# Scaling the S5 products of the output projection inside PSUM, and listing both attention outputs ahead of the recursion's second half

## The chip, the cores and the metric

The kernel runs on one core of a Trainium2 chip. The metric is the device time of one execution in microseconds (us); smaller is better. Each time below is of this one core.

## The reference, cut to what matters

A two-layer decoder trunk: 272 tokens (16 meta tokens and 256 inputs) of width 1024, float32. Each layer adds to the residual h half a SwiGLU, then a mixer, then half a SwiGLU again. The mixer projects the normalised h with `w_in`, and three groups of heads work on the columns:

- attention (256 columns): stick-breaking weights, then `o_sb = rmsnorm(weights @ v)` per head of 64;
- gated DeltaNet (256 columns): a chunked recursion over chunks of tokens, normalised per head and gated;
- S5 (512 columns): a diagonal state space model, a gate (GLU), and one rmsnorm over its 512 columns.

The three are concatenated and multiplied with `w_out` (1024 x 1024), and the product is added to h. Rows 0 to 255 of `w_out` thus belong to attention, 256 to 511 to DeltaNet and 512 to 1023 to S5. A row's rmsnorm is one factor for each token, so S5's may be applied after the product with `w_out` as well as before it.

## The kernel before, in words

Everything lies transposed: features on the 128 partitions, tokens along the free dimension. The residual is `xT` (8 blocks of 128 features by 272 tokens); the operand of each projection is held as a high and a low part, `xh` and `xl`, and the weights as `wh` and `wl`, and each product is three matmuls (`mm3`, L134 to L138): high by high (L136), low by high (L137), high by low (L138). A weight block of 512 KB is loaded by SP (L128), ScalarE makes `wh` (L130) and VectorE `wl` (L131); there are 3 buffers for the raw block, 3 for `wh` and 2 for `wl` (`NBUF`, L44).

The mixer (L1340) is a list of steps, `MIX` (L42 and L43), that the loop at L1429 walks through. It traces the instructions in this order. The framework's planner then puts them into the engines' queues by when it expects them to be ready, the earlier listed first among those that are, so a matmul listed later can stand ahead of one listed earlier that is not ready. Each queue runs in order. Buffers have tags: PSUM has four (`a` to `d`) of 2 banks each, and `cv` is an SBUF tag of 3 buffers (L857).

The letters of the list that matter here:

- `r`: one stage of the DeltaNet recursion (`dn_rest`, L1079). Stages 1 to 3 make its operands. Stages 4 and 5 are the first chunk: `pvn` (L1148), its copy (L1150), `pS` (L1154 and L1156). Stage 6 is `pk` of the second chunk (L1138 and L1139), which VectorE reads (L1142 to L1144). Stage 7 is the second chunk's `pvn` and copy, stage 8 its `pS` and the update on VectorE (L1163 to L1165), stages 9 to 11 the last 16 tokens (`pkt` L1171, `pvt` L1179 and L1183). From stage 4 on all of them use PSUM tag `d`.
- `a`: one stage of attention (`sb`, L1220). The last two are `outputs(0)` and `outputs(1)` (L1266 to L1282): six matmuls into a `d` bank (`pob`), their squares `sbr` on ScalarE (L1274), two matmuls that sum them (`pnb`, tag `c`, L1276), a root (ScalarE L101 twice, then three VectorE instructions in `newton`, L115 to L117), the scaled result `sby` (L1279) and its parts in `xh` and `xl` (L1281 and L1282). `sbr` and `sby` are `cv` buffers; the `d` bank is held until L1279 has read it.
- `x`: one half of S5's gate (`glu`, L1290). `m`: S5's factor `R5`, from a matmul of its sum of squares (`pms`, L380, tag `b`) and a root.
- `n`: ScalarE's table for Exp and Ln is loaded.
- `S4`, `S6`, `S0`, `S2`: S5's 512 rows of `w_out` for a pair of feature blocks each (`w_out_part("S", ...)`, L1402): 24 matmuls into two banks (tag `a` for S4 and S0, `b` for S6 and S2); then for each bank `sy` = product times `R5` (L1418) and its addition to `xT` (L1420).
- `o`: DeltaNet's norm and output: squares (L1191), their sum (L1193), a root, the scaled `o` (L1198), transposes `po` (L1210), `dy` (L1213 and L1215), `xh` (L1216) and `xl` (L1217) of two blocks.

After the list the four parts `Y4`, `Y6`, `Y0`, `Y2` follow (the same function with "Y"): each first the rows of attention for both banks (12 matmuls), then the rows of DeltaNet (12 more), then the addition to `xT`, from which the next SwiGLU's operand is split at once (L357).

Of the kernel before, what the change touches and what calls it, by code (L numbers as in the profile page):

```python
# [14 lines left out]
ALU = mybir.AluOpType  # L15
# [6 lines left out]
T = NMETA + SEQ  # L22
# [17 lines left out]


MIX = "C2 C3 U0 g U1 g g U2 g g g U3 g Q0 p0 p1 Q1 t0 p2 p3 K0 i t1 K1 a a t2 C0 a a i C1 i t3 a a i C4 i a a i C5 l i " \  # L42
      "y0 V0 i y1 V1 i y2 Z0 y3 Z1 v r r r r x r r x r n a r r r r a m S4 S6 o S0 S2"  # L43
NBUF = (3, 2, 3)  # L44
LO_POOL = 5

# [13 lines left out]
class Trunk:  # L60
# [1279 lines left out]
    def mixer(self, l, nxt):  # L1340
        nc, a = self.nc, self.a
        V, G, A, PE = nc.vector, nc.gpsimd, nc.scalar, nc.tensor
        w_in, w_out = a["w_in"][l], a["w_out"][l]
        t0 = NMETA if l == DEPTH - 1 else 0
        self.norm_end()
        R = self.R
        with ExitStack() as es:
            self.tmp = tmp = es.enter_context(self.tc.tile_pool(name="mix", bufs=1, reuse_waits="tile"))
            qkv = tmp.tile([P, 6, TP], F32, name="qkv")
            G.memset(qkv[:, :, T:], 0.0)  # L1350
            ba = tmp.tile([8, TP], F32, name="ba")
            G.memset(ba[:, T:], 0.0)

            def conv(b):
                src = w_in[:, 768 + b * P:768 + b * P + P]
                if b == 2:
                    p, pb = self.unit([(src, 0, P), (w_in[:, 1792:1800], P, P + 8)], P + 8, "ab")
                    V.tensor_tensor(ba[:, :T], pb[:8, :T], R[:8], op=ALU.mult)
                else:
                    p, = self.unit(src, P)  # L1360
                pad, y = self.cv("pad"), qkv[:, b, :T]
                G.memset(pad[:, 0:3], 0.0)
                V.tensor_tensor(pad[:, 3:3 + T], p[:, :T], R, op=ALU.mult)
                A.activation(y, pad[:, 0:T], AF.Copy, scale=self.cw[:, l, 0, b:b + 1])
                for k in range(1, 4):
                    V.scalar_tensor_tensor(y, pad[:, k:k + T], self.cw[:, l, k, b:b + 1], y, op0=ALU.mult, op1=ALU.add)
                if b in (2, 3):
                    self.act(y, y, AF.Silu)

            u = tmp.tile([P, 4, T], F32, name="s5u")  # L1370
            zr = tmp.tile([P, 2, T], F32, name="pz")
            q, k, v = (tmp.tile([P, 2, T], F32, name=f"p{n}") for n in "qkv")

            def s5_in(b):
                p, = self.unit(w_in[:, 1800 + b * P:1800 + b * P + P], P, "ba"[b % 2])
                i = lambda t: t.rearrange("p (c j) -> p c j", j=4)
                V.tensor_tensor(u[:, b, :].rearrange("p (j c) -> p c j", j=4), i(p[:, :T]), i(R), op=ALU.mult)

            def proj(c0, dst, b):
                p, = self.unit(w_in[:, c0 + b * P:c0 + b * P + P], P)  # L1380
                V.scalar_tensor_tensor(dst[:, b, :], p[:, :T], 0.125 if c0 == 0 else 1.0, R, op0=ALU.mult, op1=ALU.mult)

            def do_z(b):

                proj(1536, zr, b)
                t = self.cv("zt")[:, :T]
                self.act(t, zr[:, b, :], AF.Tanh, scale=0.5)
                V.scalar_tensor_tensor(zr[:, b, :], t, 1.0, zr[:, b, :], op0=ALU.add, op1=ALU.mult)

            def silu():  # L1390
                self.phase(SET_SILU)
                for b in (0, 4):
                    self.act(qkv[:, b:b + 2, :T], qkv[:, b:b + 2, :T], AF.Silu)
                self.phase(SET_GELU)

            def norms():
                self.phase(SET_LNEXP)


            rows = dict(S=((4, 5, 6, 7),), Y=((0, 1), (2, 3)))  # L1400

            def w_out_part(x, d0, tag):  # L1402
                ks = rows[x]
                lo = min(k for g in ks for k in g)
                n = sum(len(g) for g in ks)
                ps = [self.psum(tag[i % len(tag)], "proj") for i in range(2)]
                h, w = self.weights(w_out[lo * P:(lo + n) * P, d0 * P:d0 * P + 256], n, 256)
                for g in ks:
                    for j in range(2):
                        js = slice(j * P, j * P + P)  # L1410
                        for k in g:
                            self.mm3(ps[j][:, :T - t0], h[:, k - lo, js], w[:, k - lo, js],
                                     self.xh[:, k, t0:], self.xl[:, k, t0:], k == ks[0][0], k == ks[-1][-1])
                for j in range(2):
                    x_, p = self.xT[:, d0 + j, t0:], ps[j][:, :T - t0]
                    if x == "S":
                        y = self.cv("sy")[:, :T - t0]
                        V.tensor_tensor(y, p, self.R5[:, t0:], op=ALU.mult)  # L1418
                        p = y
                    V.tensor_tensor(x_, p, x_, op=ALU.add)  # L1420

            chains = dict(g=self.dn_gates(l, qkv, ba), i=self.dn_inverse(), r=self.dn_rest(qkv),
                          a=self.sb(l, q, k, v, 0), x=self.glu(l, u))
            steps = dict(C=conv, U=s5_in, Q=lambda b: proj(0, q, b), K=lambda b: proj(256, k, b), V=lambda b: proj(512, v, b),
                         Z=do_z, p=lambda r: self.s5_inputs(u, r), t=self.s5_states, y=lambda r: self.s5_outputs(u, r),
                         l=silu, v=lambda: self.sb_values(), n=norms, S=lambda d0: w_out_part("S", d0, "ab"[d0 // 2 % 2]),
                         o=lambda: (self.dn_norm(), self.dn_out(zr, self.dng[:, l], 2)),
                         m=lambda: self.rms(self.acc, 4 * 512, 0, self.R5, "b"))
            for x in MIX.split():  # L1429
                if x in chains:  # L1430
                    next(chains[x], None)
                else:
                    steps[x[0]](*(int(n) for n in x[1:]))
            assert all(next(c, 0) == 0 for c in chains.values())
            self.norm_begin(*nxt)
            for d0 in (4, 6, 0, 2):
                w_out_part("Y", d0, "ab"[d0 // 2 % 2])
                for d in {4: (4, 5), 6: (6, 7), 0: (), 2: (0, 1, 2, 3)}[d0]:
                    self.norm_block(d, d0 == 2, t0)
            self.blocks = (4, 0)  # L1440
# [42 lines left out]
```

## Time and profile before

| | before |
|---|---|
| median of 3 runs | 1169.95 us (1167.01 to 1170.87) |
| the profiled execution | 1172.42 us |
| its span in the trace | 1170.6 us |
| TensorE busy (PE) | 98% of the span |
| VectorE busy (DVE) | 73% |
| ScalarE busy (ACT) | 53% |
| mean granted TensorE clock | 0.98 of 2.4 GHz |

The profile shows one execution. PE is TensorE's matmuls, PEld its weight loads, DVE is VectorE, ACT is ScalarE, SP issues the loads from memory. A row of a timeline gives the start, the duration, engine, line, operation, what it writes and reads, the shape, how many instructions are merged in it, and in brackets how long the engine stood idle before it and what ended that. In a table of windows each engine has its busy time and its count of instructions. PEclk is the clock that TensorE was granted, as a share of 2.4 GHz: its two levels are 1.2 and 2.4 GHz, and a value between them is a mean over a stretch. The span between the trace's ends is 1.8 us shorter than the execution's own time.

### The profile page before, as it was taken

The numbers are of one execution on the slowest core, as the hardware profiler recorded it, in microseconds if no ns is written. First come the engines' busy times: TensorE is split into PE (matmuls) and PEld (weight loads), VectorE is DVE, ScalarE is ACT, GpSimd is POOL, SyncE is SP. The second block draws the span as 40 slices with busy tenths as digits, with TensorE's granted clock in tenths as the row PEclk, the third lists the DMA queues.
The fourth block names the chain that finished last, engine by engine and source line by source line (L and its number), as shares of the span: only waits on it lengthen the run. The fifth ranks groups of instructions, "written<-read, shape, count | busy, mean of one in ns | idle before, by whom it ended". The sixth has DMA issues, their size and how long they took to land.

```text
span 1170.6 us, 23740 instructions
## 1 busy us (share of the span) xinstructions
PE 1141.7 (98%) x9544; PEld 1094.8 (94%) x9544; DVE 849.4 (73%) x1621; ACT 621.7 (53%) x993; POOL 164.0 (14%) x230
## 2 busy tenths in 40 slices
PE   7999999999998999999999999999999989999997
PEld 7999999998996999999999999999989969999985
DVE  6999987589646965555569998756995578666544
ACT  6455466474653654444445555654655637555533
POOL 6411111102200011110201111011031001111100
PEclk9999999999988999999999999999999879999999
DMA  6656654642311556665566566456432216666663
GB/s 185 172 165 183 171 157 138 180 127 72 92 55 55 145 170 174 179 180 163 185 173 176 164 182 177 136 167 167 109 91 74 79 41 198 187 183 183 196 194 111
DMA packets 196859, 173.75 MB, mean 148 GB/s; under 512 B 21300, under 2 KB 193004, under 8 KB 196748
## 3 DMA queue, kind: packets, MB, share of 16 engines
q1 hardware_dynamic: 196732, 172.22, 50.4%
q8 instruction: 75, 1.23, 0.4%
q14 instruction: 36, 0.29, 0.1%
q10 hardware_dynamic: 16, 0.00, 0.0%
HBM read 171.15 MB, written 1.05 MB: 147 GB/s over the span
## 4 chain that ended last, share of the span: by engine, by line
PE 87%; DVE 6%; ACT 2%; POOL 2%; DMA 1%; issue 1%; SPq 0%; ACTq 0%; DVEq 0%; POOLq 0%
PE proj L138 18%; PE proj L136 18%; PE proj L137 18%; PE pd L138 5%; PE pd L137 5%; PE pd L136 5%; PE pd L485 5%; DVE wl L131 1%; PE pY L842 1%; POOL t L1004 1%; PE pm L775 1%; PE pinc L808 1%; PE pob L1270 1%; POOL TT L1005 1%; PE pY L840 1%
## 5 line engine op out<-in xcount | busy, mean ns | idle before, releaser
L136 PE MATMUL proj<-xh,wh 128*128 128x272 f32 (+1 forms) x1840 | 525.2, 291 | 0.8 <-DVE sy L1418 0.8
L137 PE MATMUL proj<-xl,wh 128*128 128x272 f32 (+1 forms) x1840 | 521.1, 289 | 0.0
L131 DVE TENSOR_TENSOR wl<-raw,wh 128x1024 fp32r<-128x1024 f32 (+1 forms) x324 | 392.7, 1212 | 147.2 <-PE pd L138 58.6
L138 PE MATMUL proj<-xh,wl 128*128 128x272 f32 (+1 forms) x1840 | 493.9, 291 | 2.5 <-DVE wl L131 2.3
L130 ACT ACTIVATE wh<-raw 128x1024 fp32r<-128x1024 f32 (+1 forms) x324 | 338.3, 1044 | 290.2 <-PE proj L137 86.0
L136 PEld LDWEIGHTS proj<-xh,wh 128*128 128x128 f32 x1840 | 348.8, 190 | 3.5 <-DVE sy L1418 1.6
L137 PEld LDWEIGHTS proj<-xl,wh 128*128 128x128 f32 x1840 | 348.6, 190 | 1.7
L138 PEld LDWEIGHTS proj<-xh,wl 128*128 128x128 f32 x1840 | 331.7, 189 | 5.2 <-DVE wl L131 4.0
L136 PE MATMUL pd<-hh,wh 128*128 128x272 f32 x528 | 149.6, 288 | 0.0
L137 PE MATMUL pd<-hl,wh 128*128 128x272 f32 x528 | 149.3, 288 | 0.0
L427 POOL TENSOR_TENSOR hl<-h,hh 128x272 fp32r<-128x272 f32 (+1 forms) x88 | 80.0, 911 | 455.4 <-ACT hh L426 455.3
L138 PE MATMUL pd<-hh,wl 128*128 128x272 f32 x528 | 140.7, 288 | 0.2
L136 PEld LDWEIGHTS pd<-hh,wh 128*128 128x128 f32 x528 | 99.2, 188 | 0.2
L137 PEld LDWEIGHTS pd<-hl,wh 128*128 128x128 f32 x528 | 99.2, 188 | 0.1
L138 PEld LDWEIGHTS pd<-hh,wl 128*128 128x128 f32 x528 | 95.1, 188 | 0.9 <-DVE wl L131 0.8
L101 ACT ACTIVATE g<-g 128x272 f32<-128x272 f32 (+2 forms) x92 | 37.7, 414 | 66.0 <-DVE g L421 65.7
L426 ACT ACTIVATE hh<-h 128x272 fp32r<-128x272 f32 (+1 forms) x88 | 36.4, 419 | 48.0 <-DVE h L425 48.0
L425 DVE TENSOR_TENSOR h<-proj,g 128x272 f32<-128x272 f32 (+1 forms) x88 | 37.8, 433 | 32.3 <-PE proj L138 20.8
L421 DVE TENSOR_TENSOR g<-proj,R 128x272 f32<-128x272 f32 (+1 forms) x88 | 37.5, 430 | 17.6 <-PE proj L138 17.5
L423 DVE TENSOR_TENSOR g<-g,R 128x272 f32<-128x272 f32 (+1 forms) x88 | 38.1, 436 | 13.0 <-ACT g L101 12.6
L368 POOL TENSOR_TENSOR acc<-acc,sq 128x272 f32<-128x272 f32 (+1 forms) x20 | 22.5, 1123 | 93.1 <-ACT sq L362 92.4
L485 PE MATMUL pd<-wh,hl 128*128 128x512 f32 x80 | 31.7, 396 | 0.0
(489 smaller groups left out, 1242.0 us busy)
## 6 DMA issues: line engine op xcount, KB each, us to landing
raw<-in_ffn_w_gate_dram SPq DMA_DIRECT2D x88, 512.0 KB, 3.9
raw<-in_ffn_w_up_dram SPq DMA_DIRECT2D x88, 512.0 KB, 3.8
raw<-in_ffn_w_down_dram SPq DMA_DIRECT2D x70, 512.0 KB, 3.4
raw<-in_w_in_dram SPq DMA_DIRECT2D x36, 512.0 KB, 3.8
raw<-in_ffn_w_down_dram SPq DMA_DIRECT2D x24, 384.0 KB, 2.9
raw<-in_w_out_dram SPq DMA_DIRECT2D x16, 512.0 KB, 4.0
raw<-in_s_w_glu_dram SPq DMA_DIRECT2D x4, 512.0 KB, 3.3
xin<-in_x_dram SPq DMA_DIRECT2D x4, 256.0 KB, 6.6
```

The lines of the kernel that those rows point to most:

```text
L101: i = self.nc.scalar.activation(out, in_, func, **k)
L130: nc.scalar.activation(h[:, :n], r[:, :n], AF.Copy)
L131: nc.vector.tensor_tensor(l[:, :n], r[:, :n], f32(h[:, :n]), op=ALU.subtract)
L136: mm(p, wh, xh, start=first, stop=False)
L137: mm(p, wh, xl, start=False, stop=False)
L138: mm(p, wl, xh, start=False, stop=last)
L421: V.tensor_tensor(g1, pg[j][:, :N], R, op=ALU.mult)
L423: V.tensor_tensor(g1, g1, R, op=ALU.mult)
L425: V.tensor_tensor(h, pu[j][:, :N], g1, op=ALU.mult)
L426: nc.scalar.activation(hh[:, f, :N], h, AF.Copy)
L427: G.tensor_tensor(hl[:, f, :N], h, f32(hh[:, f, :N]), op=ALU.subtract)
L485: PE.matmul(pd[i][e], x[:, f, ts], w[:, 0, e * 512:e * 512 + 512], start=f == 0 and w is h and x is hh, stop=f == NF - 1 and w is lo)
```

## The change

The list places both attention outputs directly behind the table load `n`, ahead of stages 7 to 11 of the recursion; before, `outputs(0)` stood behind stage 7 and `outputs(1)` behind stage 11. No stage is added or dropped. In the parts "S" the product with `R5` is written back into the PSUM bank that it was read from, and the addition reads that bank; the `cv` tile `sy` is gone. The count of instructions stays the same.

```diff
 MIX = "C2 C3 U0 g U1 g g U2 g g g U3 g Q0 p0 p1 Q1 t0 p2 p3 K0 i t1 K1 a a t2 C0 a a i C1 i t3 a a i C4 i a a i C5 l i " \
-      "y0 V0 i y1 V1 i y2 Z0 y3 Z1 v r r r r x r r x r n a r r r r a m S4 S6 o S0 S2"
+      "y0 V0 i y1 V1 i y2 Z0 y3 Z1 v r r r r x r r x n a a r r r r r m S4 S6 o S0 S2"
...
                     if x == "S":
-                        y = self.cv("sy")[:, :T - t0]
-                        V.tensor_tensor(y, p, self.R5[:, t0:], op=ALU.mult)
-                        p = y
+                        V.tensor_tensor(p, p, self.R5[:, t0:], op=ALU.mult)
                     V.tensor_tensor(x_, p, x_, op=ALU.add)
```

## Rows read from the trace of the kernel before

**Rows 1.** Busy time of the engines over the whole span, from the page's first part.
```profile
PE 1141.7 (98%) x9544; PEld 1094.8 (94%) x9544; DVE 849.4 (73%) x1621; ACT 621.7 (53%) x993; POOL 164.0 (14%) x230
```

**Rows 2.** Table of windows: the gap, and the stretch behind it, in both layers.
```profile
361.70:377.90 16.20, 12.13 (x89) 7.36 (x87) 8.47 (x23) 5.49 (x13) 0.29 (x1) 0.76 0.11 33
377.90:398.00 20.10, 20.09 (x152) 20.09 (x153) 19.98 (x45) 11.08 (x20) 2.67 (x3) 0.94 0.36 106
...
939.80:956.00 16.20, 12.37 (x89) 7.45 (x87) 8.56 (x23) 5.50 (x13) 0.29 (x1) 0.72 0.10 33
956.00:975.00 19.00, 19.00 (x144) 19.00 (x145) 18.24 (x42) 9.31 (x16) 2.50 (x3) 0.88 0.43 137
```

**Rows 3.** Timeline of PE in layer 0: last of S4, recursion, attention, first of S0.
```profile
354.88 0.28 PE L138 MATMUL proj<-xh,wl 128*128 128x272 f32 x1
...
361.68 1.00 PE L1148 MATMUL pvn<-ds,TTf 128*128 128x64 f32 x8
362.60 0.67 PE L1270 MATMUL pob<-W 128*64 128x272 f32 x2
...
364.73 0.45 PE L1154 MATMUL pS<-qkv,kg 128*64 128x64 f32 x8
...
366.05 0.68 PE L1276 MATMUL pnb<-sbr,bd 128*128 128x272 f32 x2
...
377.91 0.60 PE L136 MATMUL proj<-xh,wh 128*128 128x272 f32 x1 [0.42 <-DVE sy L1418]
...
380.29 0.29 PE L137 MATMUL proj<-xl,wh 128*128 128x272 f32 x1
380.42 0.29 PE L138 MATMUL proj<-xh,wl 128*128 128x272 f32 x1
```

**Rows 4.** Timeline of DVE in layer 0: R5, pk, both attention norms, sy, DeltaNet's xl.
```profile
359.07 0.44 DVE L117 SCALAR_TENSOR_TENSOR rs<-nt,rs 128x272 f32<-128x272 f32 x1
359.87 0.28 DVE L1143 TENSOR_TENSOR qkv<-pk,ex 128x128 f32<-128x128 f32 x1
...
369.87 0.50 DVE L1279 SCALAR_TENSOR_TENSOR sby<-pob,prm,sbr 128x272 f32<-128x272 f32 x1
...
375.10 0.17 DVE L115 SCALAR_TENSOR_TENSOR ot<-oR,or 128x9 f32<-128x9 f32 x1 [2.70 <-ACT or L101]
...
375.71 0.76 DVE L1198 TENSOR_TENSOR qkv<-qkv,or 128x576 f32<-128x576 f32 x1
377.07 0.44 DVE L115 SCALAR_TENSOR_TENSOR sby<-pnb,sbr 128x272 f32<-128x272 f32 x1 [0.60 <-ACT sbr L101]
377.43 0.43 DVE L1418 TENSOR_TENSOR sy<-proj,rs 128x272 f32<-128x272 f32 x1
...
380.66 0.49 DVE L1217 SCALAR_TENSOR_TENSOR xl<-dy,prm,xh 128x272 fp32r<-128x272 f32 x1
...
386.55 0.49 DVE L1217 SCALAR_TENSOR_TENSOR xl<-dy,prm,xh 128x272 fp32r<-128x272 f32 x1
```

**Rows 5.** Timeline of ACT in layer 0: copy of pvn, squares of the second attention output.
```profile
362.71 0.37 ACT L1150 COPY qkv<-pvn 128x256 f32<-128x256 f32 x1
...
374.33 0.40 ACT L1274 ACTIVATE sbr<-pob 128x272 f32<-128x272 f32 x1 [2.92 <-PE pob L1272]
```

**Rows 6.** Both instructions on an S bank, all 16 each: shortest/median/longest in ns.
```profile
L1418 DVE TENSOR_TENSOR sy<-proj,rs x16: 415/427/442, 377.4 to 964.9; 128x272 f32<-128x272 f32 x8, 128x256 f32<-128x256 f32 x8
L1420 DVE TENSOR_TENSOR xT<-sy,xT x16: 406/426/444, 378.1 to 966.7; 128x272 f32<-128x272 f32 x8, 128x256 f32<-128x256 f32 x8
```

**Rows 7.** Timeline of PE in layer 1: first of S0, and where its spacing halves.
```profile
956.00 0.58 PE L136 MATMUL proj<-xh,wh 128*128 128x256 f32 x1 [0.41 <-DVE sy L1418]
...
958.73 0.63 PE L1210 MATMUL po<-ident,qkv 128*128 128x128 f32 x2
...
959.22 0.56 PE L136 MATMUL proj<-xh,wh 128*128 128x256 f32 x1
...
960.58 0.28 PE L136 MATMUL proj<-xh,wh 128*128 128x256 f32 x1
960.70 0.28 PE L137 MATMUL proj<-xl,wh 128*128 128x256 f32 x1
```

## The prediction

> **What bounds the kernel now.** The page's first part comes first: TensorE is busy for 98% of the span [rows 1], so time can only be won where it stands still or runs slowly. The table of windows shows where that is: in 361.7 to 377.9 us of layer 0 it is busy for 12.13 of 16.20 us at a granted clock of 0.76, in the same stretch of layer 1 for 12.37 of 16.20 at 0.72; directly behind both it is busy throughout [rows 2]. Each layer thus has one hole, between the last of S6 and the first of S0. The PE timeline says what ends it: S0's first matmul waits for `sy` on VectorE, at 377.91 [rows 3].
>
> The DVE timeline says why `sy` is so late. S4's products were done at 355.2 [rows 3] and R5 at 359.5, yet the first `sy` runs at 377.43, directly behind the first write of the second attention output's `sby` at 377.07 [rows 4], although VectorE is busy for only 8.47 of the 16.20 us [rows 2]. `sbr`, `sby`, `sbr`, `sby`, `sy` is the order in which the list asks for the three `cv` buffers; so I read it as buffers of a tag given out in listed order. That `pob` starts right behind the recursion's `pvn` (361.68, 362.60) [rows 3], as the list has their `d` banks, fits this. Until `sy` runs, S4 and S6 hold all `a` and `b` banks, and S0, S2 and Y can't start, though S0's and S2's weights are ready.
>
> **The change part by part.** *The product in PSUM.* It removes no instruction: 16 multiplications and 16 additions stay. It removes the `cv` request, so S4 can be scaled when R5 is there (359.5) and VectorE has a place, about 361, and S0 can start some 16 us earlier. The write into PSUM is in no row. Above, I bound it by the dearest row on 272 columns that also reads a bank, L1279 with 0.50 [rows 4] against 0.43: 16 x 0.07 = 1.1 us of VectorE. Below, I see no reason against a small gain, and take the same size with the other sign. I take nothing, since the instruction that reads a bank (427 ns) and the one that reads only SBUF (426 ns) are equal [rows 6], and VectorE has 7.7 us free in the hole. The bank is held for one more instruction; the next group in it waits 0.4 us longer, which the other tag's group covers; without that cover it is 8 x 0.4 = 3 us a layer. The Trainium skill, "Perfetto Trace Analysis", section Optimizing Scalar/DVE Operations, gives VectorE an access cost of about 60 ns on SBUF and 125 on PSUM. By that, an estimate from that page, the 16 additions would cost 1.0 us more on VectorE; rows 6 show no such difference between the two places for a read.
>
> *The outputs in front.* What moves is 2 x 6 `pob` and 2 x 2 `pnb` matmuls, on ScalarE 8 instructions, on VectorE 10; no DMA, nothing on POOL or SP. On SP the later `w_out` loads come earlier, as VectorE frees raw blocks earlier. `pk` was read out at 359.87 + 0.28 = 360.15 [rows 4], so `pob` starts at 360.2, not 362.60. Its norm took until 369.87 + 0.50 = 370.37, that is 7.8 us; 1.3 of these are `pS`, which stood ahead of `pnb` from 364.73 to 366.05 [rows 3, 4]. So the first `d` bank comes free at 360.2 + 6.5 = 366.7.
>
> *The wait that this adds.* With banks in listed order both `d` banks belong to attention until then, and stage 7 starts at 366.7 instead of 361.68, 5.0 us later. Behind it on TensorE stand only S, Y and its own successors; ScalarE's copy, `pS` and all of DeltaNet's output wait for it. From `pvn` to the scaled `o` it took 361.68 to 375.71 + 0.76 = 376.47: 14.8 us. Of these the moved work cost 1.6 (the copy ended at 363.08, `pS` came at 364.73 behind `pob`) [rows 3, 5] and some 2.2 (a wait of 2.70 for the root, in which ScalarE sat behind the second output's squares at 374.33; the root's own 0.45 off) [rows 4, 5]; both go. The second output's bank holds `pS` up by about 0.8. So `o` is scaled at 366.7 + 14.8 - 3.8 + 0.8 = 378.5. From there to the first `xl` of DeltaNet it took 4.7 (376.47 to 381.15); the second came at 387.04 only because it ranked low on a full VectorE [rows 4]. I take 4.5 for both: DeltaNet's rows are there at **383** in layer 0. The distance of the layers is 956.00 - 377.91 = 578.1 [rows 3, 7], so 961.1 in layer 1.
>
> *What TensorE does meanwhile.* S0 and S2 (48 matmuls, 6 us) and the attention halves of Y4 and Y6 (24, 3 us), whose inputs are now early, fill the hole; the fixed work in it fits beside them. What is left at 383 is 96 - 24 = 72 matmuls. A matmul takes 0.13 us in layer 0 by the rows at 380.29 and 380.42, I take 0.125, and 0.12 in layer 1 [rows 3, 7]. Before, TensorE had 144 matmuls (S0, S2 and Y) from 377.91 on: ten to 380.29, then 134 x 0.125 and 0.24 for `po`: end at 397.3. In layer 1, 19 to 960.58, then 125 x 0.12: 975.6. Now: 383 + 72 x 0.125 = 392.0 and 961.1 + 72 x 0.12 = 969.7. Gain 5.3 + 5.9 = 11.2 us.
>
> *The clock.* Before, S0's first matmuls still ran at 1.2 GHz, 2.38 - 10 x 0.125 = 1.1 us too slow in layer 0 and 4.58 - 0.49 (`po`) - 19 x 0.12 = 1.8 us in layer 1 [rows 3, 7], after a hole that was busy for three quarters [rows 2]. Now the tail of the recursion is thin between about 373 and 383, so I charge the same to Y. **Sum: -11.2 + 2.9 = -8.3 us.** VectorE doesn't bound the end: it was busy for 19.98 of 20.10 us behind the hole [rows 2], but 16 S instructions of about 0.4 and the second attention norm, some 8 us, move forward into its free time.
>
> The profiled execution took 1172.42 us, its span 1170.6; minus 8.3 that is 1164.1 and 1162.3. It lies 2.5 above the median of 1169.95, for which I give **1161.6**.
>
> **The rivals.** *Only half of the fill.* Y4's weights need a `wl` buffer that S0 gives back, and ScalarE and VectorE are in the norms just then. If the planner leaves Y's attention halves behind DeltaNet's, 96 matmuls stay: ends at 395.0 and 972.6, gain 2.3 + 3.0, less the clock's 2.9: 2.4, or 1167.5. For it: until now no Y matmul had to run ahead of DeltaNet's rows, so no row shows that it will. Against: VectorE has room in the hole [rows 2].
>
> *Slower: the recursion comes too late.* The place is stage 7 behind attention's banks. If none of the 3.8 us come back and the second `xl` again trails `o` by 10.6 us (376.47 to 387.04) [rows 4], it is there at 366.7 + 14.8 + 10.6 = 392.1; with 69 matmuls behind it the end is 400.7, 3.4 later, and 978.5 in layer 1, 2.9 later: 1176.3. It decides from where the second `xl` comes after 397.3 - 69 x 0.125 = 388.7. For it: the old trace shows such a trail. Against: the trail stood behind S's 16 instructions, which now run earlier.
>
> *The change does not do what it says.* If `sy` was late for its rank in VectorE's queue and not for its buffer, S0 stays behind the norms; attention's second norm ends earlier but DeltaNet later: about 0, 1170. Against: VectorE idles for 2.70 us right before [rows 4].
>
> *The hole closes entirely.* Without the clock's 2.9 us and with DeltaNet's rows 1.4 us earlier in each layer it is -14, 1156.
>
> **How the numbers follow.** A measurement of this kernel can tell about 0.3% from no change, 3.5 us. Chances: forecast 0.60 and closed hole 0.04, both faster; half fill 0.16, which lies near the bound, 0.06 of it faster and 0.10 the same; no effect 0.09, the same; late recursion 0.11, slower. That makes faster 0.70, same 0.19, slower 0.11. The range runs from the closed hole, 1156, to the half fill with 0.5 for the unknown write into PSUM, 1168; outside lie no effect and late recursion, 0.20.
>
> **What would show it.** Right: `pob` twice in a row at about 360, stage 7 at about 367, the scaling of S4 at about 361 and S0's matmuls between 362 and 375; PE busy in 361.7 to 377.9 for over 15 us; L1418 still near 427 ns; the second DeltaNet `xl` near 383. Wrong: S0 still waiting for L1418 after 370; the second `xl` after 388.7; VectorE full and TensorE idle behind 383; L1418 over 0.5 us.

## The result: slower by 0.9%, and the profile after

The change takes 1182.0 us (median of 12 runs, 1172.85 to 1189.52) against 1171.8 for the kernel before, measured beside it: ratio **1.0087, 95% interval 1.0059 to 1.0116**. The forecast was 8 us faster; it is 10 us slower, and the rival "the recursion comes too late" had the right sign. The two profiled executions show nearly the same loss where the change sits: from the first `pk` to the end of the last addition it takes 45.3 us in layer 0 and 45.8 in layer 1, against 41.0 and 40.7 before, together 9.5 us more. Traces are compared by their distance from `pk` below, since the executions reach `pk` at different times (358.53 and 936.74 before, 355.84 and 940.02 after).

Part 1 of the page, after; it answers to [rows 1]:

```profile
span 1179.5 us, 23731 instructions
PE 1144.8 (97%) x9544; PEld 1099.0 (93%) x9544; DVE 847.7 (72%) x1621; ACT 621.4 (53%) x993; POOL 165.9 (14%) x230
```

The table of windows, after, for the stretches that answer to [rows 2] (the same distance from `pk` as there in layer 0 and behind it, then in layer 1; columns as in that group):

```profile
359.00:375.20 16.20, 15.36 (x106) 12.95 (x105) 11.52 (x26) 6.06 (x11) 0.00 (x0) 0.96 0.30 93
375.20:395.30 20.10, 14.23 (x104) 12.61 (x104) 11.59 (x31) 6.79 (x15) 0.73 (x2) 0.78 0.06 11
943.10:959.30 16.20, 14.05 (x96) 11.95 (x95) 11.98 (x27) 6.75 (x12) 0.00 (x0) 0.94 0.34 103
959.30:978.30 19.00, 12.94 (x99) 11.40 (x99) 9.25 (x27) 4.34 (x10) 0.29 (x1) 0.69 0.06 24
```

The old hole is closed as forecast: TensorE is busy for 15.36 of 16.20 us, where it was 12.13, and at a clock of 0.96 for 0.76. But behind it, where it had been busy throughout, it now stands for 5.9 us in layer 0 and 6.1 in layer 1, at 0.78 and 0.69. The hole has moved back, and has grown.

The timeline of PE, after (first the layer 0 rows that answer to [rows 3], then two of layer 1, [rows 7]):

```profile
355.84 0.43 PE L1138 MATMUL pk<-qkv,kn 64*128 64x64 f32 x2
...
359.08 0.67 PE L1270 MATMUL pob<-W 128*64 128x272 f32 x2
...
361.20 0.67 PE L1270 MATMUL pob<-W 128*64 128x272 f32 x2
...
365.07 0.62 PE L1276 MATMUL pnb<-sbr,bd 128*128 128x272 f32 x2
...
369.68 0.62 PE L1276 MATMUL pnb<-sbr,bd 128*128 128x272 f32 x2
370.98 1.07 PE L1148 MATMUL pvn<-ds,TTf 128*128 128x64 f32 x8 [0.43 <-DVE sby L1279]
...
384.22 1.09 PE L1210 MATMUL po<-ident,qkv 128*128 128x128 f32 x4 [4.09 <-DVE qkv L1198]
...
386.85 1.27 PE L136 MATMUL proj<-xh,wh 128*128 128x272 f32 x4 [1.12 <-ACT xh L1216]
...
956.39 1.08 PE L1148 MATMUL pvn<-ds,TTf 128*128 128x64 f32 x8 [2.15 <-DVE sby L1279]
...
969.23 1.09 PE L1210 MATMUL po<-ident,qkv 128*128 128x128 f32 x4 [4.09 <-DVE qkv L1198]
```

Stage 7 (`pvn`) comes 15.1 us behind `pk` (16.4 in layer 1), where it had been 3.2, and what it waits for is L1279: attention's read of its `d` bank. At the other end `po` waits 4.09 us for the norm of `o`, and Y's first DeltaNet rows another 1.12, with nothing beside them. These waits are the new hole.

The timeline of DVE, after, layer 0, which answers to [rows 4] (two rows in front of L1144, then the root of attention's first output, then DeltaNet's output):

```profile
357.39 1.14 DVE L1417 TENSOR_TENSOR proj<-proj,rs 128x272 f32<-128x272 f32 x3
...
358.82 1.13 DVE L1418 TENSOR_TENSOR xT<-proj,xT 128x272 f32<-128x272 f32 x3
359.87 0.42 DVE L1144 TENSOR_TENSOR ds<-vb,ds 128x256 f32<-128x256 f32 x1
...
366.71 0.44 DVE L115 SCALAR_TENSOR_TENSOR sby<-pnb,sbr 128x272 f32<-128x272 f32 x1 [0.64 <-ACT sbr L101]
367.10 0.45 DVE L1417 TENSOR_TENSOR proj<-proj,rs 128x272 f32<-128x272 f32 x1
367.46 1.22 DVE L131 TENSOR_TENSOR wl<-raw,wh 128x1024 fp32r<-128x1024 f32 x1
368.59 0.44 DVE L116 SCALAR_TENSOR_TENSOR sby<-sby,sbr 128x272 f32<-128x272 f32 x1
368.95 0.43 DVE L1418 TENSOR_TENSOR xT<-proj,xT 128x272 f32<-128x272 f32 x1
369.30 0.44 DVE L1417 TENSOR_TENSOR proj<-proj,rs 128x272 f32<-128x272 f32 x1
369.65 0.43 DVE L117 SCALAR_TENSOR_TENSOR sbr<-sby,sbr 128x272 f32<-128x272 f32 x1
370.00 0.43 DVE L1418 TENSOR_TENSOR xT<-proj,xT 128x272 f32<-128x272 f32 x1
370.35 0.49 DVE L1279 SCALAR_TENSOR_TENSOR sby<-pob,prm,sbr 128x272 f32<-128x272 f32 x1
...
383.31 0.76 DVE L1198 TENSOR_TENSOR qkv<-qkv,or 128x576 f32<-128x576 f32 x1
...
387.00 1.06 DVE L1217 SCALAR_TENSOR_TENSOR xl<-dy,prm,xh 128x272 fp32r<-128x272 f32 x2
```

S4 is scaled early, 1.6 us behind `pk`, as the reading of the `cv` buffers had it. The price stands in the same rows: the S5 work, early now, lies between the links of the root that the `d` bank waits for. DeltaNet's last `xl` ends 32.2 us behind `pk` (28.5 before).

The writes into PSUM cost nothing that counts. The lines of the product and of the addition, after:

```profile
L1417 DVE TENSOR_TENSOR proj<-proj,rs x16: 421/435/450, 357.4 to 954.3; 128x272 f32<-128x272 f32 x8, 128x256 f32<-128x256 f32 x8
L1418 DVE TENSOR_TENSOR xT<-proj,xT x32: 411/428/443, 358.8 to 985.4; 128x272 f32<-128x272 f32 x16, 128x256 f32<-128x256 f32 x16
```

Before it was 427 ns for the product and 426 for the addition that read `sy` [rows 6]: 16 x (8 + 2) ns = 0.16 us over both layers. The Trainium skill, "Perfetto Trace Analysis", section Optimizing Scalar/DVE Operations, gives an access of VectorE about 60 ns on SBUF and about 125 on PSUM. The 65 ns between the two, an estimate from that page, do not show in these rows: they have 8 and 2 ns.

### The profile page after: what moved, and what is told of

Same layout as the page of the kernel before. It is cut to its first block, busy times and chain, and to the rows that moved or that the text cites. A ratio compares the mean times of both kernels' runs of the same rounds, so it can differ in the third digit from the quotient of the medians.

```text
span 1179.5 us, 23731 instructions
## 1 busy us (share of the span) xinstructions
PE 1144.8 (97%) x9544; PEld 1099.0 (93%) x9544; DVE 847.7 (72%) x1621; ACT 621.4 (53%) x993; POOL 165.9 (14%) x230
## 4 chain that ended last, share of the span: by engine, by line
PE 84%; DVE 8%; ACT 2%; issue 2%; POOL 2%; DMA 2%; SPq 0%; ACTq 0%; DVEq 0%; POOLq 0%
PE proj L138 17%; PE proj L136 17%; PE proj L137 17%; PE pd L138 5%; PE pd L137 5%; PE pd L136 5%; PE pd L485 5%; DVE wl L131 2%; PE pY L842 1%; POOL t L1004 1%; PE pm L775 1%; PE pinc L808 1%; POOL TT L1005 1%; PE pY L840 1%; DVE xl L357 1%
## 5 line engine op out<-in xcount | busy, mean ns | idle before, releaser
L101 ACT ACTIVATE g<-g 128x272 f32<-128x272 f32 (+2 forms) x92 | 37.7, 415 | 62.2 <-DVE g L421 62.1
L426 ACT ACTIVATE hh<-h 128x272 fp32r<-128x272 f32 (+1 forms) x88 | 36.5, 420 | 47.7 <-DVE h L425 47.5
L421 DVE TENSOR_TENSOR g<-proj,R 128x272 f32<-128x272 f32 (+1 forms) x88 | 37.5, 430 | 16.9 <-PE proj L138 16.7
L423 DVE TENSOR_TENSOR g<-g,R 128x272 f32<-128x272 f32 (+1 forms) x88 | 38.1, 436 | 12.8 <-ACT g L101 12.4
L485 PE MATMUL pd<-wh,hl 128*128 128x512 f32 x80 | 31.6, 396 | 0.0
```

What stands on the lines that cost most here:

```text
L101: i = self.nc.scalar.activation(out, in_, func, **k)
L421: V.tensor_tensor(g1, pg[j][:, :N], R, op=ALU.mult)
L423: V.tensor_tensor(g1, g1, R, op=ALU.mult)
L426: nc.scalar.activation(hh[:, f, :N], h, AF.Copy)
L485: PE.matmul(pd[i][e], x[:, f, ts], w[:, 0, e * 512:e * 512 + 512], start=f == 0 and w is h and x is hh, stop=f == NF - 1 and w is lo)
```

## The experiments

Theories: **A**, stage 7 waits because attention's two outputs hold both `d` banks through a norm. **B**, the S5 work, set free early, stands ahead of the small links of the recursion and of the norms in the queues of TensorE and VectorE. **C**, from the second group on, is B with its other side: what is used up there is missing beside the norm of `o`. **D**, the product in PSUM costs by itself. Ratios are to the kernel before, measured beside each on the same chip. The distances are from one trace each, layer 0 / layer 1, in us behind the first `pk`: stage 7, the end of the last operand row of Y (the last of L1217 and L1282), the end of the last addition.

| kernel | ratio, 95% interval | stage 7 | last rows | last addition |
|---|---|---|---|---|
| before | 1 | 3.2 / 3.0 | 28.5 / 28.2 | 41.0 / 40.7 |
| the change | 1.0087 (1.0059 to 1.0116) | 15.1 / 16.4 | 32.2 / 33.0 | 45.3 / 45.8 |
| e1_inplace | 1.0058 (1.0034 to 1.0081) | 6.8 / 6.6 | 31.6 / 31.7 | 45.8 / 45.4 |
| e2_order | 1.0083 (1.0048 to 1.0117) | 11.3 / 11.2 | 35.6 / 34.8 | 49.1 / 47.5 |
| e3_pob_c | 0.9986 (0.9962 to 1.0011) | 5.7 / 5.6 | 25.5 / 25.1 | 39.2 / 37.5 |
| e4_old_pob_c | 1.0005 (0.9978 to 1.0032) | 5.7 / 5.6 | 25.5 / 25.6 | 39.2 / 38.1 |
| e5_old_late | 1.0089 (1.0054 to 1.0123) | 2.7 / 2.7 | 33.1 / 31.5 | 45.9 / 43.4 |
| e6_new_late | 1.0078 (1.0045 to 1.0111) | 9.9 / 10.0 | 34.5 / 34.2 | 46.0 / 45.0 |
| e7_oldc_late | 1.0051 (1.0024 to 1.0077) | 4.9 / 4.3 | 28.7 / 27.3 | 40.3 / 38.2 |
| e8_rec_first | 1.0124 (1.0093 to 1.0156) | 2.7 / 2.7 | 33.1 / 30.3 | 46.7 / 43.5 |
| e9_inplace_late_parts | 1.0006 (0.9978 to 1.0035) | 3.2 / 3.0 | 28.2 / 27.9 | 41.3 / 40.2 |
| e10_inplace_s6 | 0.9990 (0.9967 to 1.0014) | 3.4 / 3.3 | 27.1 / 27.3 | 40.1 / 40.8 |
| e11_second_behind_r8 | 0.9994 (0.9971 to 1.0018) | 3.2 / 3.0 | 28.3 / 28.3 | 40.3 / 39.5 |
| e12_pob_c_only | 1.0053 (1.0035 to 1.0071) | 5.3 / 5.6 | 26.4 / 25.3 | 40.1 / 37.7 |
| e13_one_front | 1.0048 (1.0022 to 1.0073) | 5.4 / 5.2 | 30.6 / 32.7 | 42.5 / 43.8 |
| e14_one_front_inplace | 1.0005 (0.9979 to 1.0030) | 8.8 / 8.5 | 28.4 / 28.1 | 41.7 / 39.3 |
| e15_r8_inplace_s6 | 1.0009 (0.9982 to 1.0037) | 3.4 / 3.3 | 28.9 / 30.3 | 40.8 / 41.4 |
| e16_one_front_s6 | 0.9963 (0.9937 to 0.9989) | 5.7 / 5.6 | 27.6 / 27.9 | 39.6 / 39.0 |

In e3, e4, e7 and e12 the distances flatter: `pob` runs before `pk` there, which comes some 3 to 6 us later in the layer for it. And each trace is of one execution, which need not be the median one: that of e6 took 1191.83 us against a median of 1181.25, that of e2 1190.44 against 1184.73. So e2's distances, 14.9 us more than before over both layers, overstate its loss, which is 9.7 us by the ratio.

**First group: each half alone, and the banks.** e1 is the change with the old list, e2 the new list with the product through `cv`:

```diff
# e1, against the change
-      "y0 V0 i y1 V1 i y2 Z0 y3 Z1 v r r r r x r r x n a a r r r r r m S4 S6 o S0 S2"
+      "y0 V0 i y1 V1 i y2 Z0 y3 Z1 v r r r r x r r x r n a r r r r a m S4 S6 o S0 S2"
# e2, against the kernel before
-      "y0 V0 i y1 V1 i y2 Z0 y3 Z1 v r r r r x r r x r n a r r r r a m S4 S6 o S0 S2"
+      "y0 V0 i y1 V1 i y2 Z0 y3 Z1 v r r r r x r r x n a a r r r r r m S4 S6 o S0 S2"
# e3, against the change; e4, against e1
-            po = self.psum("d", "pob")
+            po = self.psum("c", "pob")
```

> The product in PSUM alone, with the list of before. Theory A (the changed kernel is slow because attention's outputs, listed in front, hold both d banks and so push the recursion's second half behind their norms): stage 7 starts again within 4 us of the end of pk's reading, S0 and S2 fill the hole, the second DeltaNet xl comes before the decision point: 0.991 to 0.996 of before. Theory B (S's work on TensorE and VectorE, set free early by the product in PSUM, stands ahead of the small links of attention and recursion and delays them whatever the list says): no faster than before, 1.000 to 1.006.

1.0058, in B's range: each half loses alone, and the losses don't add up (0.58% here, 0.83% in e2, 0.87% together). Stage 7 comes 6.8 us behind `pk` instead of 3.2, though no attention output stands in front: on PE, 38 S matmuls lie between `pk` and stage 7, where 12 had been, 26 x 0.125 = 3.3 us. Used up there, they are missing at the end (e1, PE, in front of Y; and the window before it):

```profile
378.70:381.70 3.00, 0.04 (x1) 0.00 (x0) 2.79 (x8) 0.94 (x2) 0.00 (x0) 0.87 0.00 0
```

```profile
381.76 0.60 PE L136 MATMUL proj<-xh,wh 128*128 128x272 f32 x1 [3.02 <-ACT xh L1281]
```

> The new list alone, with sy in its cv buffer as before. Theory A: stage 7 still waits for attention's d banks, DeltaNet's rows are late as in the changed kernel: 1.004 to 1.010 of before. Theory B: no S0 matmul can stand ahead of pnb, since S0 waits for a cv buffer, so the norms and then stage 7 come about 4 us earlier than in the changed kernel, S0 and S2 fill what follows: 0.993 to 0.999.

1.0083, in A's range. Without any early S5 work stage 7 still waits for attention's first norm; TensorE stands, and `pvn` takes 1.97 us behind it where the change has 1.07 (e2, PE):

```profile
363.96 0.73 PE L1276 MATMUL pnb<-sbr,bd 128*128 128x272 f32 x2
...
367.77 1.97 PE L1148 MATMUL pvn<-ds,TTf 128*128 128x64 f32 x8 [1.03 <-DVE sby L1279]
```

> The changed kernel with pob in a bank of tag c instead of d, so that the recursion does not wait for attention's norms. Theory A: stage 7 within 4 us of pk, TensorE idle for less than 3 us in the hole: 0.989 to 0.996 of before. Theory B: the small links are still behind S matmuls: 1.003 to 1.010, as the changed kernel.

0.9986: outside both ranges, and the whole loss of the change is gone with one letter. It is not a clean test of A, though: the first `pob` now starts 22 us ahead of `pk`.

> The product in PSUM, the list of before, and pob in tag c. Theory A: at least as fast as the product in PSUM alone, 0.988 to 0.995 of before, since neither chain waits for the other's bank. Theory B: 1.000 to 1.006.

1.0005 in B's range: against e1 the early S5 work costs nothing here, with attention's norms out of the way.

**Second group: the S5 work held back.** If early S5 work is what hurts (C), a later `R5` should heal it. `m` moves behind stage 9 and takes a `d` bank, in all four:

```diff
# e5 to e8, against the change
-                         m=lambda: self.rms(self.acc, 4 * 512, 0, self.R5, "b"))
+                         m=lambda: self.rms(self.acc, 4 * 512, 0, self.R5, "d"))
# e5; e7 has the same list, and pob in tag "c"
+      "y0 V0 i y1 V1 i y2 Z0 y3 Z1 v r r r r x r r x r n a r r m r r a S4 S6 o S0 S2"
# e6
+      "y0 V0 i y1 V1 i y2 Z0 y3 Z1 v r r r r x r r x n a a r r r m r r S4 S6 o S0 S2"
# e8
+      "y0 V0 i y1 V1 i y2 Z0 y3 Z1 v r r r r x r r x r n r r m r r a a S4 S6 o S0 S2"
```

> In-place product, the old list but for m, which moves from behind the second attention output to behind stage 9 and takes a d bank: R5 and with it S0, S2 come only when the first part of the recursion's end (pkt) is out. Theory C (the S5 work, once it is free early, is put ahead of the recursion's links and is then missing beside the norm of o): stage 7 about 3 us behind pk and o scaled about 18 us behind pk as in the kernel before, S0 and S2 beside the norms of the second output and of o, ratio 0.991 to 0.999. Theory D (the product in PSUM costs by itself, by its write or by the bank that it holds): as e1_inplace, 1.004 to 1.010. Theory A (only the d banks of attention's outputs matter): as before, 1.000.

1.0089: a miss for C, and in D's range. Stage 7 came 2.7 us behind `pk`, but the last rows 33.1 instead of 28.5. The trace shows part of why (e5, PE, attention's first output, and a window over it and what follows; in the change the same `pob` took 0.67):

```profile
363.69 1.17 PE L1270 MATMUL pob<-W 128*64 128x272 f32 x2
...
365.59 1.17 PE L1270 MATMUL pob<-W 128*64 128x272 f32 x2
```

```profile
363.60:375.40 11.80, 9.86 (x57) 5.98 (x56) 3.75 (x11) 2.47 (x7) 0.00 (x0) 0.50 0.01 2
```

With no S5 work beside the chain the granted clock fell to 0.50, its lower level, and the chain's own matmuls took nearly twice as long. So fill was not only in the way; without any, the links themselves got slower. It is not a clean test of C, though: the edit also puts `m` among the users of the `d` banks. The second output's `pob` started at 376.30, right behind the last read of `pms` (L115, until 376.24), and the root of `R5` ran between the recursion's last links. How much of the loss is the clock's and how much is `m`'s stays open, here and in e6 to e8.

> The change itself, but m behind stage 9 and in a d bank, so that S0 and S2 come late. Theory A: both d banks are still attention's, stage 7 some 8 to 11 us behind pk and PE idle in that wait, since nothing fills it; o scaled about 24 to 26 us behind pk. With C the fill then stands beside the norm of o: ratio 1.000 to 1.007, between e5 and the change. If A's wait costs nothing by itself: as e5, under 1.000. Theory D: 1.008 and more.

1.0078, just under D's range and just over A's with C. Stage 7 is at 9.9, as A has it, and the S5 work held back buys little.

> As e5_old_late, and pob in a c bank, so that attention's outputs wait for no d bank and their norms are done before the recursion's end. Theory C and A together: o scaled some 15 to 17 us behind pk, S0 and S2 beside its norm, ratio 0.985 to 0.995. Theory D: 1.002 and more (e4_old_pob_c had 1.0005 with the early R5). If attention's outputs, moved ahead of pk, only push pk back by what they save, 0.997 to 1.001.

1.0051 against e4's 1.0005: holding the S5 work back, with `m` in a `d` bank, costs here too. C's range is missed; D's is hit, but e9 speaks against D.

> In-place product, m behind stage 9 in a d bank, and both attention outputs behind the recursion's last stage. Theory A: the recursion's banks are free of attention, o scaled 14 to 17 us behind pk, DeltaNet's rows 3 to 5 us earlier than before; attention's rows come last, about 24 us behind pk, and S0, S2 cover them: ratio 0.990 to 1.000. If attention's two norms, now at the end, become the last thing that Y waits for: 1.003 and more. Theory D: 1.004 and more.

1.0124, the case with attention's norms last, and also in D's range: `o` is early (its scaled rows 18.4 us behind `pk`), and Y waits for attention's rows at 33.1. But that is not all: DeltaNet's own second `xl` came only 0.4 us ahead of them, 14 us behind the scaled `o`, with S5 instructions and attention's second norm between on VectorE. The trace accounts for 8.5 of the 14.5 us; its execution was 4.3 us faster than the median, and the rest is open.

**Third group: the write alone, half the dose, another place.**

```diff
# e9, against the kernel before; e10 with (6,) for (0, 2)
-                        y = self.cv("sy")[:, :T - t0]
+                        y = p if d0 in (0, 2) else self.cv("sy")[:, :T - t0]
# e11, against the kernel before
+      "y0 V0 i y1 V1 i y2 Z0 y3 Z1 v r r r r x r r x r n a r a r r r m S4 S6 o S0 S2"
# e12, against the kernel before
-            po = self.psum("d", "pob")
+            po = self.psum("c", "pob")
```

> The kernel before, with the product in PSUM for S0 and S2 alone; S4 and S6, whose banks decide when S0 and S2 start, keep their cv tile. Every step stands where it stood. Theory D (the write into PSUM or the longer held bank costs by itself): 8 of 16 products, so half of e1_inplace's loss or more, 1.002 to 1.005. Theory C (only the earlier start of S0 and S2 counts): 0.998 to 1.002, stage 7 about 3 us and o about 17 us behind pk as before.

1.0006 (0.9978 to 1.0035), and the distances are those of before. D falls as the main cause: half of e1's loss would have been 1.0029, which the interval still holds, but nothing in the rows pays for it.

> The kernel before, with the product in PSUM for S6 alone: S2 (24 matmuls) may come early, S0 stays behind the second sby and covers the norm of o. Theory C with the clock (the fill must neither stand ahead of stage 7 nor be missing at the end, and without any of it beside the chain the clock falls): half a dose beside the recursion and half behind it, 0.994 to 1.001. If each early S matmul costs what it delays: half of e1_inplace, 1.001 to 1.005.

0.9990 against e1's 1.0058, the same list: 24 early matmuls instead of 48, only 14 S matmuls instead of 38 in front of stage 7, and the loss is gone. C's range holds it, that of half of e1's loss doesn't. It fits that the amount put ahead of the links is what costs.

> The kernel before, product through cv, with the second attention output moved from behind stage 11 to behind stage 8: its second sby, and so sy, come earlier, S0 and S2 start after the recursion's last links instead of before them, and stage 7 waits for no attention bank. Theory C: stage 7 3 us behind pk as before, stages 9 to 11 about 3 us later for pob and its bank, S0 and S2 from about 14 us behind pk on, beside the norm of o: 0.992 to 1.000. Theory A in its strong form (each attention output ahead of a link costs its whole norm): 1.003 and more.

0.9994, in C's range, no gain that can be told.

> The kernel before with pob in a c bank and nothing else. Attention's outputs wait for no d bank and are done before the recursion's end, so that sy comes early without the product in PSUM. If the gain of e3_pob_c over the change (0.9986 against 1.0087) is all from the banks: 0.995 to 1.001 here too, stage 7 5 to 6 us behind pk. If the product in PSUM is what keeps e3_pob_c and e4_old_pob_c at par: 1.003 and more.

1.0053, so the product in PSUM does help e3 and e4. Their traces don't show where: from the first `pk` on they are within 0.9 us of e12 in both layers. That stays open.

**Fourth group: the bank alone, and the version that follows.** Only the first output stays in front, so that one `d` bank is left for stage 7.

```diff
# e13, e14, e16, against the kernel before
+      "y0 V0 i y1 V1 i y2 Z0 y3 Z1 v r r r r x r r x n a r r a r r r m S4 S6 o S0 S2"
# e13: product through cv; e14: all products in PSUM, as in the change
# e15: the list of e11; e15 and e16: product in PSUM for S6 alone
+                        y = p if d0 in (6,) else self.cv("sy")[:, :T - t0]
```

> e2_order with only the first attention output ahead of stage 7 and the second behind stage 8; product through cv. Theory A (stage 7 waits because both outputs hold both d banks): stage 7 comes 5 to 6.5 us behind pk instead of 11.3, o is scaled 22 to 25 us behind pk instead of 31, ratio 0.993 to 1.001 against 1.0083. If it is not the bank but the outputs' place in the queues that costs: stage 7 still 8 us or more behind pk, 1.004 and more.

Stage 7 at 5.4 instead of 11.3, as A said. Six `pob` less in front account for about 2.1 us of this (359.08 to 361.20 in the change); the rest, an estimated 3.8, is the wait for the bank. The ratio, 1.0048, missed A's range. With `sy` late the S5 work is set free in one lump in front of the norm of `o`, whose rows come at 30.6 and 32.7.

> e13 with all products in PSUM, that is the change with its second output behind stage 8. Theory A alone: under 1.001, as e13. Theory C (early S0 and S2 stand ahead of the links): what e1_inplace lost is lost here too, 23 matmuls ahead of stage 7 and 24 ahead of pS, o 25 us or more behind pk, 1.002 to 1.008.

1.0005 against the change's 1.0087, with the second output's place as the only difference. Stage 7 moves from 15.1 to 8.8 and no longer waits for L1279 (e14, PE):

```profile
367.81 0.62 PE L1276 MATMUL pnb<-sbr,bd 128*128 128x272 f32 x2
368.26 1.00 PE L1148 MATMUL pvn<-ds,TTf 128*128 128x64 f32 x8
```

So with the S5 work early, two outputs in front instead of one are worth the whole loss; with it late the same move is worth less (e2's 1.0083 to e13's 1.0048). Here too A's and B's shares don't add up. C's range is missed: early S5 work (e14) is better than late (e13) in this list.

> e10 and e11 together: second output behind stage 8, product in PSUM for S6 alone. If the two gains add: pk to the last addition 38.5 to 39.5 us, 0.994 to 0.999. If they are one gain (the same fill cannot be used twice): 0.998 to 1.002.

1.0009: e10 and e11 don't add.

> e13 with the product in PSUM for S6 alone: 24 early matmuls, most of them behind stage 7. Theory C: between e13 and e14, 0.996 to 1.003; stage 7 6 us behind pk.

**0.9963 (0.9937 to 0.9989)**, 1168.5 us against 1173.5, in C's range: faster than both kernels, though it is the best of sixteen variants and was measured once. Stage 7 comes at 5.7, the root of attention's first output runs through without S5 work between its links, half the S5 work lies beside the recursion and half beside the norm of `o` (e16, DVE):

```profile
367.11 0.44 DVE L115 SCALAR_TENSOR_TENSOR sby<-pnb,sbr 128x272 f32<-128x272 f32 x1 [2.98 <-ACT sbr L101]
367.59 0.44 DVE L116 SCALAR_TENSOR_TENSOR sby<-sby,sbr 128x272 f32<-128x272 f32 x1
368.06 0.44 DVE L117 SCALAR_TENSOR_TENSOR sbr<-sby,sbr 128x272 f32<-128x272 f32 x1
368.62 0.50 DVE L1279 SCALAR_TENSOR_TENSOR sby<-pob,prm,sbr 128x272 f32<-128x272 f32 x1
...
380.07 0.76 DVE L1198 TENSOR_TENSOR qkv<-qkv,or 128x576 f32<-128x576 f32 x1
```

The table also shows what sets the end: in all 18 kernels and both layers the last addition ends 10.8 to 14.2 us behind the last rows, which themselves come 25.1 to 35.6 us behind `pk`. Filling a hole ahead of these rows moves the end mainly by where it leaves them.

## Why the prediction was wrong

**What held.** `sy`'s buffer was what kept S0 back; the S5 work and both `pob` ran early; the old hole is busy for 15.36 us; L1418 kept its price. From `pvn` to the scaled `o` it took 13.1 us (12.7 in layer 1) for 11.8 forecast, from there to the second `xl` 4.0 for 4.5. Y's end behind its last rows, with the clock's charge and the 2.2 us from the last matmul to the end of the last addition, should have been 12.3 and 12.6 us and was 13.1 and 12.7. The clock's term had the right cause and was somewhat small: from the second `xl` on, TensorE ran at 0.50 for 2.74 and 4.83 us, which costs half of it, 1.4 and 2.4 us where 1.1 and 1.8 were charged. Against it, 67 matmuls were left in either layer instead of 72.

**The step that failed** is "So the first `d` bank comes free at 360.2 + 6.5 = 366.7", 8.2 us behind `pk`. It was free at 15.0 and, in layer 1, at 16.2. That one term carries most of the miss: 6.8 and 8.0 of the 17.8 us between the forecast of -8.3 and the +9.5 of the traces. By it DeltaNet's rows, forecast 24.5 and 24.4 us behind `pk`, came at 32.2 and 33.0, in sum 16.4 us late. In layer 0, three things were missing in it:

- `pob` did not start when `pk` had been read out, 1.7 us behind `pk`, but at 3.2: the 12 matmuls of S6 stand in front of it. **1.5 us**; e2 shows the same 3.2 without any early S5 work.
- The second output's six `pob` stand ahead of the first `pnb`. The first output's squares were done at 361.31 + 0.40 = 361.71 (row below), the second's `pob` at 363.3: **1.6 us**. I had counted the moved instructions for the second bank, and let the first norm run as if it were alone.
- "The fixed work in it fits beside them" was the deeper error. The fill did not lie beside the chain of small links; it stood between them, in the queues of TensorE and VectorE. 13 matmuls of S0 took from 363.3 to about 365.0 in front of `pnb`, **1.7 us**, and four S5 instructions and a weight split stood in the root's way on VectorE: its three steps took 3.64 us to L1279 (366.71 to 370.35) and 1.51 where nothing was between them (e16, 367.11 to 368.62), **2.1 us**.

The first two, 3.1 us, come with the list alone, as A's wait does, and e2 has them alone: stage 7 at 11.3, just that much behind the forecast. The last two, 3.8 us, are B, and just what lies between e2's 11.3 and the change's 15.1. In layer 1 B costs 5.2 (11.2 to 16.4). The timeline of ACT, after, between `pob` and `pnb`:

```profile
361.31 0.40 ACT L1274 ACTIVATE sbr<-pob 128x272 f32<-128x272 f32 x1 [1.19 <-PE pob L1272]
...
365.73 0.49 ACT L101 ACTIVATE sbr<-pnb,eps 128x272 f32<-128x272 f32 x1 [4.02 <-PE pnb L1276]
```

**Where the expected gain went.** The 72 matmuls of S0, S2 and Y's attention halves did run early. But TensorE had not lacked work behind the hole before: when the second `xl` was done, at 387.04, it had (397.3 - 387.04) / 0.125, about 82 of the 144 matmuls, left [rows 3, 4], against the 72 of the forecast. That is 1.2 us (2.0 in layer 1, where 89 were left behind 964.95); S0, S2 and Y's halves had covered the norm of `o` already. The other 7.9 of the 11.2 us of gain could come only from earlier DeltaNet rows, and those came later. Now the fill was spent ahead of and between the links, the waits of 4.09 and 1.12 us for `o` were left bare, and Y began at the lower clock.

**The rival** "the recursion comes too late" named the place, stage 7 behind attention's banks, and its point of decision held: the second `xl` after 388.7, 30.2 us behind `pk`, means slower; it came at 32.2 and 33.0. Its mechanism was only half right. The trail from `o` to `xl`, to which it gave 10.6 us, vanished (4.0); the delay sat in front of stage 7. That its sign was right was in part luck. I gave it 0.11, for lack of adding up what stands in TensorE's queue between `pob` and `pnb`.

## What to carry to other kernels

A hole in front of a chain of small dependent steps is closed by moving work only if the chain's end does not move; work out when the chain ends, with every instruction that the planner may put between its links, before counting what fills the hole. A bank held through a norm makes the step that wants it next wait for the whole norm (e2): put only as many producers in front as leave that step a bank (e13, e14). And spread the fill: here too much of it delayed the links (e1), with none of it the clock fell (e5), and some had to be left for the tail.

## What the runs showed of the hardware

Not expected was a fall of the clock with TensorE full. In 325 to 345 us, far ahead of the change, the profiled kernel before has it and e1 does not (windows of the kernel before, then of e1). In the 20 us ahead of that window TensorE had been busy throughout at a clock of 1.00 in both. The other sixteen traces show the fall in the same part of layer 0 too; only e1's lacks it.

```profile
325.00:345.00 20.00, 20.00 (x153) 19.25 (x152) 8.79 (x16) 10.71 (x23) 1.80 (x1) 0.74 0.17 54
```

```profile
325.00:345.00 20.00, 19.79 (x175) 18.81 (x175) 12.48 (x26) 15.49 (x30) 1.81 (x1) 1.00 0.23 75
```

The same stretch of a layer, from the first `pz` (L1246) to the first `pk`, takes 80.1 us in the one and 75.4 in the other, both in layer 0. A difference of 5 us between two single traces can be this alone, so that only distances within the changed stretch, or medians of many runs, tell of the change. What made the clock fall there stays open.
